# Letting the scan's tree stages in by VectorE's backlog, with ScalarE's bookings, two buffers, two loads and one product changed

## The chip, the cores and the metric

One core of a Trainium2 chip runs the kernel. The metric is the device time of one execution in microseconds; shorter is better. The engines are TensorE (PE, with PEld for its weight loads), VectorE (DVE), ScalarE (ACT), GpSimd (POOL) and the DMA queues, of which SyncE's (SP) carries nearly all loads.

## The reference

One encoder layer on 256 tokens with a model width of 2048, all in float32:

```python
h = rmsnorm(x, norm_mix_pre)
q_na, k_na, v_na, u_ssm, q_mem = split(h @ w_in)        # 1024, 1024, 1024, 512, 512 columns
y_na  = neighbourhood_attention(q_na, k_na, v_na, rpb)  # 8 heads x 128
y_ssm = s5_mixer(u_ssm, ...)                            # 32 groups x 64 complex states, forward and backward
y_mem = memory_cross_attention(q_mem, mem, mem_norm, w_mem_kv)   # 4 heads x 128, 256 memory tokens
y = concat(rmsnorm(y_na), rmsnorm(y_ssm), rmsnorm(y_mem))
x = x + rmsnorm(y @ w_out, norm_mix_post)
x = x + rmsnorm(square(relu(rmsnorm(x, norm_mlp_pre) @ w_ff1)) @ w_ff2, norm_mlp_post)   # hidden 8192
```

`s5_mixer` scans `h[t] = a * h[t-1] + b u[t]` over the tokens in both directions for each state, takes `Re(C h)` summed over the directions, adds `d * u`, and ends in a GELU and a gate `y * sigmoid(y @ w_glu + b_glu)` (the GLU).

## The kernel before

**The weight stream.** All weight matrices are cut into blocks of 128x128 and laid out in the order of use; eight blocks make a chunk (512 KB). For each chunk SyncE's queue loads `wraw`, ScalarE rounds it to the high part `wh` (`conv_high`), and VectorE subtracts to get the low part `wl` (`conv_low`). TensorE multiplies high by high, high by low and low by high. `take` (line 331) hands out blocks. At the start of a chunk it has the chunk two ahead converted (`AHEAD` = 2), and that in turn has a load issued; raw chunks have three buffers. Engines run their queues in order.

**The planner.** The kernel's Python code fixes the order of every queue while it writes the program. Side work (attention heads, the SSM, norms) is written as tasks, generators that issue a few instructions and then yield. `book` (line 109) keeps a clock for VectorE ("V"), GpSimd ("G"), ScalarE ("A") and TensorE ("E"), to which each instruction adds a booked cost (the `call` in `Engine`, line 128). `tick` (line 243), called at the start and in the middle of each chunk, goes through the tasks by priority and lets one step as long as it is due and each engine that it uses is booked less than `BACK` ns ahead of TensorE. `drain` forces a task to its end where its result is needed at once.

**The SSM** (lines 500 to 880). `lam_task` makes the discretised eigenvalues and their powers on VectorE and GpSimd. For each of four groups of channels `ut`, `b_task` runs `prep_b`, which makes powers of B (tile `W`, one buffer), transposes them (`wx`, `W1T`) and has `incr` multiply them with the inputs; the result for direction `d` is written to `XS`, and (`ut`, `d`) joins `xs_part`. `c_task` runs `prep_c`: it loads `Cw`, makes powers of C on VectorE and copies them to `CC` on ScalarE. `k0_task` then issues small matmuls on `CC`. `tree_task` runs `tree` twice, for groups 0 and 1 and for groups 2 and 3. A tree is the scan, in place in `XS`, in eleven stages of four VectorE instructions; the stages at level `l` touch columns that lie 2 to the power `l` + 1 apart, and their width falls from 32 columns to 1 and grows again. `ssm_task` issues the output matmuls and the GELU of each group (`ssm_out`) and then `yH` and `yL`, the GLU's input, which must be there after the first of four column groups of the output projection.

In the kernel before, the buffer with tag `ps` serves both `Cw` and the tree's temporary. `in_c` and `in_tree` keep `c_task` and `tree_task` from running together.

**The norm after the mix.** Near 440 us `r1`, the reciprocal root, is made (`rsqrt_pool`). `x1_part` adds the normed projection `acc1` to `x1` in column parts: on VectorE for the first 256 columns, and on ScalarE (product) and GpSimd (sum) for the others, the last quarter eight steps later. `gpost` holds the norm's weights, with which GpSimd multiplies `acc1`, quarter by quarter.

Of the kernel before, what the change touches and what calls it, by code (L numbers as in the profile page):

```python
# [41 lines left out]
SH_G = 500.0  # L42
BACK_V, BACK_G, BACK_A = 2600.0, 4000.0, 2200.0
WARM0, WARM1 = 7, 10
# [57 lines left out]
def hybrid_kernel(ctx: ExitStack, tc: tile.TileContext, A: dict, out: bass.AP, dbg=None):  # L102
# [16 lines left out]
    class Engine:  # L119
# [3 lines left out]
        def __getattr__(self, name):  # L123
# [3 lines left out]
            def call(o, *a, **kw):  # L127
# [11 lines left out]
                elif name == "tensor_reduce":  # L139
                    c = 80 + 1.04 * a[0].shape[1] * a[0].shape[2]  # L140
                elif e == "A":
                    c = 100 + 0.83 * n + (95 if any(isinstance(x, bass.AP) for x in kw.values()) else 0)
                elif e == "V":
                    c = (72 if n > 64 else 140) + n * {"tensor_copy": 0.52, "reciprocal": 8.0, "tensor_tensor_scan": 1.04,
                                   "tensor_scalar": 0.76, "memset": 0.3}.get(name, 1.04)
                else:
                    c = 155 + n * {"tensor_scalar": 0.9, "memset": 0.0, "tensor_copy": 1.6}.get(name, 2.1)
# [73 lines left out]
    tasks = []  # L221
    BACK = dict(V=BACK_V, G=BACK_G, A=BACK_A)

# [19 lines left out]
    def tick():  # L243
        for t in list(tasks):
            more = t[2] <= clk["E"]
            while more and all(clk[e] - clk["E"] < BACK[e] for e in t[3]):
                more = step(t)
# [444 lines left out]
    def incr(ut, d, wt):  # L692
# [8 lines left out]
        c0 = 8 * (ut % 2) + 4 * d  # L701
        o = XS[ut // 2][:, :, c0:c0 + 4, :]
        act(o[:, :, :, ::-1] if d else o, X)
        xs_part.add((ut, d))
# [7 lines left out]
    def prep_c(ut):  # L712
        cw = a2.tile([128, 4, 2, 8, 16], F32, name="Cw", tag="ps", bufs=1)
        nc.sync.dma_start(cw[:, 0], A["c"][:, ut])
# [37 lines left out]
    def tree(g):  # L752
# [3 lines left out]
        for up, l in [(1, l) for l in range(LEV)] + [(0, l) for l in range(LEV - 2, -1, -1)]:  # L756
# [3 lines left out]
            dst, src = X[:, :, :, d0::2 * h], X[:, :, :, d0 - h:NB - h:2 * h]  # L760
            t = a2.tile([128, 2, 16, NB // 2], F32, name="ps", tag="ps", bufs=1)[:, :, :, 0:n]
            tt(V, t, src[:, ::-1], pw[:, l, 0:2, cols][:, :, :, None].to_broadcast([128, 2, 16, n]), mult)
            tt(V, dst, dst, t, add)
# [55 lines left out]

    in_c, in_tree = [], []  # L820

    def b_task():
# [4 lines left out]
    def c_task():  # L827
        yield from until(lambda: lam_done)
        for ut in range(4):
            yield from until(lambda: not in_tree and (ut < 2 or ut - 2 in out_done))  # L830
            in_c.append(ut)
            yield from prep_c(ut)
            prepc.add(ut)
            in_c.clear()

    def tree_task():
        for g in range(2):
            yield from until(lambda: pw_done and not in_c and (2 * g + 1, 1) in xs_part and len(prepc) >= 2)
            in_tree.append(g)
            yield from tree(g)  # L840
            in_tree.clear()
            trees.add(g)
# [67 lines left out]
    for ut in range(2):  # L910
        load_b(ut)
    spawn(lam_task("V"), 2, "V")
    spawn(b_task(), 3, "VA")
    spawn(c_task(), 3, "VA")
    spawn(k0_task(), 3, "VA")
    spawn(tree_task(), 4, "V")
    st = spawn(ssm_task(), 5, "GA")
# [288 lines left out]
    rsqrt_pool(r1, v1)  # L1206
    for t in range(2):
        a = acc1[:, t, quarter(3)]
        tt(G, a, a, gpost[3], mult)
    B = ExitStack()  # L1210
# [4 lines left out]
    def x1_part(c):  # L1215

        for t in range(2):
            if c.stop <= 256:
                stt(x1[:, t, c], acc1[:, t, c], r1[:, t:t + 1], x1[:, t, c], mult, add)
            else:  # L1220
                act(acc1[:, t, c], acc1[:, t, c], AF.Copy, scale=r1[:, t:t + 1])
                tt(G, x1[:, t, c], x1[:, t, c], acc1[:, t, c], add)
# [270 lines left out]
```

## Time and profile before

| | |
|---|---|
| median of 3 runs | 1174.77 us (1172.07 to 1175.4) |
| the profiled execution | 1176.17 us, of which the span from first to last instruction is 1174.4 |
| TensorE busy | 1129.9 us, 96% of the span |
| VectorE busy | 718.5 us, 61% |
| ScalarE busy | 588.7 us, 50% |
| GpSimd busy | 97.7 us, 8% |
| mean granted TensorE clock | 0.987 of full speed |

The span falls into the first projection (to about 60 us), the memory keys and values (to about 114), the attention projections with the SSM beside them (to about 335), the output projection (to 440) and the MLP. A row of the timeline has the start, the duration, the engine, the instruction, what it writes and reads, and in brackets how long the engine sat idle before it and what ended that.

### The profile page before, as it was taken

What the parts mean: (1) busy time and instruction counts of PE and PEld (TensorE: products, weight loads), DVE (VectorE), ACT (ScalarE), POOL (GpSimd) and SP (SyncE); (2) the same over time, 40 slices, a digit from 0 to 9 for tenths busy, and PEclk for the clock granted to TensorE, in tenths of its full rate; (3) what the DMA queues carried; (4) which work ended last, traced back from release to release, by engine and by line L of the source; (5) the groups of instructions that cost most, each with busy time, mean ns of one, the idle gap of its engine ahead of it and who ended that gap; (6) DMA issues with size and microseconds to landing.
All of it is one profiled execution on the core that took longest, in us unless ns stands there. A gap on an engine that the chain in (4) does not pass through costs nothing.

```text
span 1174.4 us, 17404 instructions
## 1 busy us (share of the span) xinstructions
PE 1129.9 (96%) x6776; PEld 976.4 (83%) x6776; DVE 718.5 (61%) x1060; ACT 588.7 (50%) x908; POOL 97.7 (8%) x161
## 2 busy tenths in 40 slices
PE   8989896999989998999999999999999999999996
PEld 7978796989878887888888888888888888888885
DVE  6767498566966766676665444445666665445454
ACT  5677643566455546555455434343444544344342
POOL 1750000010000034000000000000000000011011
PEclk9999998999999999999999999999999999999998
DMA  8875353344444684666666666666666666666673
GB/s 285 303 218 171 109 162 104 100 131 138 154 127 142 187 280 145 182 190 188 195 187 189 186 191 184 191 185 192 189 190 194 186 192 184 193 193 197 189 210 127
DMA packets 62723, 213.05 MB, mean 181 GB/s; under 512 B 7216, under 2 KB 8752, under 8 KB 62640
## 3 DMA queue, kind: packets, MB, share of 16 engines
q1 hardware_dynamic: 62352, 211.84, 58.6%
q8 instruction: 53, 0.87, 0.3%
q14 instruction: 30, 0.25, 0.1%
q10 hardware_dynamic: 288, 0.09, 0.0%
HBM read 209.81 MB, written 2.10 MB: 180 GB/s over the span
## 4 chain that ended last, share of the span: by engine, by line
PE 72%; DVE 3%; issue 1%; ACT 1%; POOL 0%; DVEq 0%; ACTq 0%; POOLq 0%
PE acc L149 66%; PE big L149 5%; PE att L149 2%; DVE wl L149 1%; DVE ps L149 1%; DVE XS L149 1%; POOL x L149 0%; DVE facc L149 0%; ACT CC L149 0%; ACT wh L149 0%; DVE mn L149 0%; DVE rt L149 0%; DVE P L149 0%; DVE r L149 0%; ACT yH L149 0%
## 5 line engine op out<-in xcount | busy, mean ns | idle before, releaser
L149 DVE TENSOR_TENSOR wl<-wraw,wh 128x1024 fp32r<-128x1024 f32 (+1 forms) x372 | 454.2, 1225 | 389.2 <-ACT wh L149 389.0
L149 ACT ACTIVATE wh<-wraw 128x1024 fp32r<-128x1024 f32 (+1 forms) x372 | 391.2, 1054 | 419.4 <-PE acc L149 303.5
L149 PE MATMUL acc<-hs,wh 128*128 128x512 f32 (+1 forms) x996 | 346.4, 391 | 0.0
L149 PE MATMUL acc<-hs,wl 128*128 128x256 f32 x992 | 279.8, 283 | 0.0
L149 PEld LDWEIGHTS acc<-hs,wh 128*128 128x128 f32 x996 | 187.1, 188 | 38.6 <-ACT hs L149 0.2
L149 PEld LDWEIGHTS acc<-hs,wl 128*128 128x128 f32 x992 | 187.9, 190 | 0.0
L149 PE MATMUL acc<-wh,fH 128*128 128x512 f32 x448 | 178.8, 399 | 0.0
L149 PE MATMUL acc<-wh,fL 128*128 128x512 f32 x448 | 176.7, 394 | 0.0
L149 PE MATMUL acc<-wl,fH 128*128 128x512 f32 x448 | 175.7, 392 | 0.0
L149 PEld LDWEIGHTS acc<-wh,fL 128*128 128x128 f32 x448 | 84.1, 188 | 21.8
L149 PEld LDWEIGHTS acc<-wl,fH 128*128 128x128 f32 x448 | 84.1, 188 | 20.1
L149 PEld LDWEIGHTS acc<-wh,fH 128*128 128x128 f32 x448 | 84.1, 188 | 19.2
L149 PE MATMUL acc<-xH,wl 128*128 128x256 f32 x256 | 74.8, 292 | 9.3 <-DVE wl L149 9.2
L149 PE MATMUL acc<-xH,wh 128*128 128x256 f32 x256 | 77.2, 301 | 4.4 <-ACT wh L149 4.4
L149 PE MATMUL acc<-xL,wh 128*128 128x256 f32 x256 | 74.0, 289 | 0.0
L149 PEld LDWEIGHTS acc<-xH,wl 128*128 128x128 f32 x256 | 50.6, 198 | 10.6 <-DVE wl L149 10.6
L149 PEld LDWEIGHTS acc<-xH,wh 128*128 128x128 f32 x256 | 50.8, 199 | 5.2 <-ACT wh L149 4.6
L149 PEld LDWEIGHTS acc<-xL,wh 128*128 128x128 f32 x256 | 50.7, 198 | 0.4
L149 POOL TENSOR_TENSOR facc<-facc,g 128x512 f32<-128x512 f32 x6 | 10.1, 1710 | 475.5 <-DMA g<-in_g_dram 475.5
L149 PE MATMUL acc<-wh,mixn 128*128 128x512 f32 x128 | 40.8, 396 | 0.0
L149 ACT ACTIVATE P<-P,mn 128x256 f32<-128x256 f32 x24 | 12.0, 501 | 40.8 <-DVE mn L149 40.8
L149 DVE TENSOR_TENSOR XS<-XS,ps 128x32 f32<-128x32 f32 (+9 forms) x44 | 29.1, 661 | 1.5
(305 smaller groups left out, 1503.0 us busy)
## 6 DMA issues: line engine op xcount, KB each, us to landing
wraw<-in_w_dram SPq DMA_DIRECT2D x369, 512.0 KB, 4.3
tokst<-in_xt_dram SPq DMA_DIRECT2D x4, 512.0 KB, 7.9
mst<-in_memT_dram SPq DMA_DIRECT2D x4, 512.0 KB, 4.6
tokst<-in_mt_dram SPq DMA_DIRECT2D x4, 512.0 KB, 6.3
bias<-in_bias_dram SPq DMA_DIRECT2D x8, 256.0 KB, 4.0
x<-in_xt_dram SPq DMA_DIRECT2D x8, 256.0 KB, 5.9
out_dram<-facc SPq DMA_DIRECT2D x8, 256.0 KB, 2.4
xst<-in_xT_dram SPq DMA_DIRECT2D x7, 256.0 KB, 7.4
```

Source lines behind the costliest of these rows:

```text
L149: return f(o, *a, **kw)
```

## The change

- A tree stage may enter while VectorE is booked less than 1700 ns ahead (`BACK_TREE`, key `v`) instead of 2600, and stages above level 0 book `4 * 32 * n` ns more, `n` being their columns.
- ScalarE's booked costs go up: 205 ns instead of 100 per instruction, 80 for a scale from memory or a bias, 186 for an accumulator. Its limit `BACK_A` goes from 2200 to 3000.
- For groups 2 and 3 `Cw` lies in the buffer of `W`, `c_task` waits for (3,1) in `xs_part`, and the exclusion of `c_task` and `tree_task` is gone.
- The loads of B for groups 0 and 1 are issued ahead of the weights of chunks 5 and 6 instead of ahead of everything.
- The last quarter's product with `gpost[3]` moves from two GpSimd instructions into `x1_part`, where VectorE multiplies by `r1` and `gpost[3]` at once in place of ScalarE's product by `r1`.
- The output of `act` in `incr` is written in another form with the same meaning.

```diff
-BACK_V, BACK_G, BACK_A = 2600.0, 4000.0, 2200.0
+BACK_V, BACK_G, BACK_A, BACK_TREE = 2600.0, 4000.0, 3000.0, 1700.0
...
                 elif e == "A":
-                    c = 100 + 0.83 * n + (95 if any(isinstance(x, bass.AP) for x in kw.values()) else 0)
+                    c = (205 + 0.83 * n + (80 if isinstance(kw.get("scale"), bass.AP) or "bias" in kw else 0)
+                         + (186 if "accum_out" in kw else 0))
...
-    BACK = dict(V=BACK_V, G=BACK_G, A=BACK_A)
+    BACK = dict(V=BACK_V, G=BACK_G, A=BACK_A, v=BACK_TREE)
...
-            while more and all(clk[e] - clk["E"] < BACK[e] for e in t[3]):
+            while more and all(clk[e.upper()] - clk["E"] < BACK[e] for e in t[3]):
...
-        o = XS[ut // 2][:, :, c0:c0 + 4, :]
-        act(o[:, :, :, ::-1] if d else o, X)
+        act(XS[ut // 2][:, :, c0:c0 + 4, ::-1 if d else 1], X)
...
-        cw = a2.tile([128, 4, 2, 8, 16], F32, name="Cw", tag="ps", bufs=1)
+        cw = a2.tile([128, 4, 2, 8, 16], F32, name="Cw", tag="ps" if ut < 2 else "W", bufs=1)
...
             t = a2.tile([128, 2, 16, NB // 2], F32, name="ps", tag="ps", bufs=1)[:, :, :, 0:n]
+            if l:
+                book("V", 4 * 32 * n)
...
-            yield from until(lambda: not in_tree and (ut < 2 or ut - 2 in out_done))
-            in_c.append(ut)
+            yield from until(lambda: ut < 2 or ut - 2 in out_done and (3, 1) in xs_part)
...
-            yield from until(lambda: pw_done and not in_c and (2 * g + 1, 1) in xs_part and len(prepc) >= 2)
-            in_tree.append(g)
+            yield from until(lambda: pw_done and (2 * g + 1, 1) in xs_part and len(prepc) >= 2)
...
     for ut in range(2):
-        load_b(ut)
+        at(before_dma, 5 + ut, load_b, ut)
...
-    spawn(tree_task(), 4, "V")
+    spawn(tree_task(), 4, "v")
...
     rsqrt_pool(r1, v1)
-    for t in range(2):
-        a = acc1[:, t, quarter(3)]
-        tt(G, a, a, gpost[3], mult)
...
-                act(acc1[:, t, c], acc1[:, t, c], AF.Copy, scale=r1[:, t:t + 1])
+                if c.start >= 1536:
+                    stt(acc1[:, t, c], acc1[:, t, c], r1[:, t:t + 1], gpost[3], mult, mult)
+                else:
+                    act(acc1[:, t, c], acc1[:, t, c], AF.Copy, scale=r1[:, t:t + 1])
```

## Rows read from the trace of the kernel before

**Rows 1.** Waits of TensorE in the whole span: total, times, longest, in us.

```profile
PE acc L149 <- DVE wl L149: 12.7, 10, 3.6
```

**Rows 2.** Busy time by stage; columns PE, PEld, DVE, ACT, POOL, clock, DMA.

```profile
60.00:150.00 90.00, 82.57 (x538) 70.67 (x537) 58.93 (x124) 64.71 (x125) 15.64 (x48) 0.98 0.52 160
150.00:200.00 50.00, 39.59 (x300) 37.92 (x299) 48.33 (x73) 23.10 (x39) 0.73 (x1) 0.92 0.41 127
200.00:285.00 85.00, 82.65 (x825) 75.97 (x824) 46.78 (x95) 51.96 (x102) 6.59 (x9) 0.97 0.41 128
285.00:334.00 49.00, 43.54 (x319) 41.33 (x316) 47.10 (x68) 21.97 (x41) 0.74 (x1) 0.97 0.43 144
```

**Rows 3.** Timeline of TensorE: its longest waits between 60 and 440 us.

```profile
136.28 0.91 PE L149 MATMUL att<-CC,W 128*32 128x96 f32 x32 [2.53 <-issue]
...
193.84 0.58 PE L149 MATMUL acc<-xH,wh 128*128 128x256 f32 x1 [4.36 <-ACT wh L149]
...
198.27 0.58 PE L149 MATMUL acc<-xH,wl 128*128 128x256 f32 x1 [3.64 <-DVE wl L149]
...
265.59 0.91 PE L149 MATMUL att<-CC,W 128*32 128x96 f32 x32 [2.35 <-ACT CC L149]
...
325.15 0.54 PE L149 MATMUL acc<-xH,wl 128*128 128x256 f32 x1 [3.33 <-DVE wl L149]
```

**Rows 4.** Busy time and granted clock (third column from the end) behind two waits.

```profile
198.30:202.40 4.10, 4.10 (x19) 4.10 (x20) 2.33 (x4) 1.71 (x4) 0.00 (x0) 0.51 0.59 197
267.40:270.70 3.30, 3.30 (x15) 3.01 (x14) 0.00 (x0) 3.25 (x9) 0.00 (x0) 0.51 0.39 130
```

**Rows 5.** Timeline of ScalarE in the first tree.

```profile
191.74 0.51 ACT L149 ACTIVATE P<-P,mn 128x256 f32<-128x256 f32 x1 [9.99 <-DVE mn L149]
...
192.74 2.94 ACT L149 ACTIVATE wh<-wraw 128x1024 fp32r<-128x1024 f32 x3
```

**Rows 6.** Timeline of VectorE in the first tree.

```profile
191.62 1.18 DVE L149 TENSOR_TENSOR ps<-XS,pw 128x992 f32<-128x992 f32 x1
...
197.00 3.49 DVE L149 TENSOR_TENSOR wl<-wraw,wh 128x1024 fp32r<-128x1024 f32 x3
```

**Rows 7.** The page's costliest groups: busy us, mean ns; half of both trees.

```profile
L149 DVE TENSOR_TENSOR XS<-XS,ps 128x32 f32<-128x32 f32 (+9 forms) x44 | 29.1, 661 | 1.5
```

**Rows 8.** Groups of instructions by shape, VectorE, 60 to 380 us: a narrower stage.

```profile
L149 DVE TENSOR_TENSOR ps<-XS,pw 128x512 f32<-128x512 f32 x4 | 4.3, 1084 | 0.1
```

**Rows 9.** The chain that ended last: start, us, what.

```profile
272.78 11.45 PE acc L149 x96
```

**Rows 10.** Groups of instructions by shape, ScalarE, whole span.

```profile
L149 ACT ACTIVATE wh<-wraw 128x1024 fp32r<-128x1024 f32 x369 | 389.8, 1058 | 419.1 <-PE acc L149 303.5 <-issue 70.1 <-DMA wraw<-in_w_dram 33.7
```

**Rows 11.** Timeline of ScalarE: the last increment, (3,1), is written.

```profile
272.81 0.60 ACT L149 ACTIVATE XS<-att 128x512 f32<-128x512 f32 x1 [1.64 <-PE att L149]
```

**Rows 12.** Timeline of VectorE: the last instruction of the second tree.

```profile
331.13 1.19 DVE L149 TENSOR_TENSOR XS<-XS,ps 128x992 f32<-128x992 f32 x1
```

**Rows 13.** Timeline of TensorE: the GLU begins.

```profile
376.92 0.39 PE L149 MATMUL acc<-yH,wl 128*128 128x256 f32 x1 [0.39 <-DVE wl L149]
```

**Rows 14.** Timeline of SyncE's DMA queue: its first row.

```profile
0.72 0.86 SPq L648 DMA_DIRECT2D W<-in_b_dram  x2
```

**Rows 15.** The chain that ended last, from 446 us on.

```profile
446.49 1.43 POOL x L149 x2
```

**Rows 16.** Timeline of all engines ahead of the MLP.

```profile
441.24 0.16 DVE L149 TENSOR_TENSOR rt<-ry 128x2 f32<-128x2 f32 x1 [0.84 <-POOL ry L149]
441.31 2.48 POOL L149 TENSOR_TENSOR acc<-acc,gpost 128x512 f32<-128x512 f32 x2
441.44 1.15 DVE L149 SCALAR_TENSOR_TENSOR rt<-rt,v 128x2 f32<-128x2 f32 x1
442.62 1.19 DVE L149 SCALAR_TENSOR_TENSOR r<-rt,ry 128x2 f32<-128x2 f32 x1
...
444.25 1.26 PE L149 MATMUL att<-ident,x 128*128 128x128 f32 x4 [2.94 <-DVE x L149]
```

**Rows 17.** Timeline of GpSimd: the last quarter's sums.

```profile
465.54 2.54 POOL L149 TENSOR_TENSOR x<-x,acc 128x512 f32<-128x512 f32 x2 [6.72 <-ACT acc L149]
```

## What the change is expected to do

> **What bounds the kernel now.** I read first who TensorE waited for [rows 1], then its busy time by stage [rows 2], then the long waits one by one [rows 3], then the granted clock behind them [rows 4]. The reader should see that TensorE is the bound and that it waits mostly for `wl`, the low parts that VectorE makes. Its idle time by stage is 90.00 − 82.57 = 7.4 us in 60 to 150 us, 10.4 us in 150 to 200, 2.4 us in 200 to 285 and 5.5 us in 285 to 334 [rows 2]. The two stretches with the most idle time are those in which VectorE is full: 48.33 of 50 us and 47.10 of 49 us. Between them, from 200 to 285 us, VectorE is busy for only 46.78 of 85 us [rows 2]. VectorE's work is not too much; it lies badly.
>
> The two full stretches are the two runs of `tree`. The chain in the first is short to follow. A ScalarE softmax instruction waits 9.99 us for the minimum `mn`, which stands behind tree stages in VectorE's queue; the conversions `wh` of three chunks stand behind it on ScalarE and start only at 192.74 us [rows 5]. On VectorE a whole tree stage (four instructions from 191.62 us) comes next and the three `wl` start at 197.00 us [rows 6]. TensorE, two chunks on, waits 4.36 us and then 3.64 us; in the second tree 3.33 us [rows 3]. After these waits the granted clock is 0.51, the lower of the two levels (1.2 GHz), for 4.1 us with TensorE busy throughout; there are five such stretches, of 3.3 to 4.1 us, each behind a wait [rows 4].
>
> **Why the trees pile up.** The planner lets a tree stage in while VectorE's booked backlog is under 2600 ns. A stage is four instructions, booked at 72 + 1.04 n each (140 where n is at most 64). For n = 512 that is 604 ns, and the trace has 1084 [rows 8]. (This n counts elements; the code's own counts columns, 32 elements each.) Summing the eleven stages (n = 1024, 512, 256, 128, 64, 32, 32, 96, 224, 480, 992), the booking is 20.0 us a tree. The trace has 29.1 us for half of the instructions of both trees, the other half having the same shapes, so about 29 us a tree [rows 7]. Some 9 us a tree are on VectorE and in no booking.
>
> **Trees (line 762 and the gate).** The added booking is 128 ns per column for every level but 0; the columns of those stages sum to 57, so 7.3 us, and a tree is booked at 27.2 us: 2 us short instead of 9. A stage is now let in under 1700 ns. Bound for what stays: a chunk takes about 2.8 us of TensorE (24 matmuls; 96 of them took 11.45 us [rows 9]), and `wl` is wanted two chunks, 5.6 us, after it is queued. In the worst case a stage enters half a chunk (1.4 us) ahead of that: 1.7 + 4 × 1.23 − 1.4 + 1.23 = 6.5 us, so 0.7 us late allowing 0.2 us for the matmuls ahead of the first `wl`. The 512 and 480 stages come to about 0.2 us. Four of each kind give at most 3.6 us, at least nothing. What can go: 10.4 + 5.5 us of idle [rows 2], and of the lower clock about half of 4.1 us and half of an alike stretch of 3.3 us behind 325.15 us, 3.6 us; 19.5 us in all. I take 17.5, near the middle of 15.9 and 19.5.
>
> **ScalarE's bookings and BACK_A.** Two waits stand at `k0` (2.53 and 2.35 us [rows 3]): its matmuls are queued when the planner thinks the C powers are copied into `CC`, and ScalarE is later than booked. Booking 105 ns more for each plain instruction and 186 for an accumulator moves `k0` back by perhaps 1 us. With the clock behind them (half of 3.4 us and of 3.3 us) these waits cost 4.9 + 3.3 = 8.2 us. Between 0 and 8.2 I take 3.0: the planner also books these small matmuls too dear on TensorE, and that is not touched. BACK_A rises from 2200 to 3000, so with the new bookings steps come in about as often as before.
>
> **The C powers in the B buffer** (tag `W` for groups 2 and 3). `c_task` and `tree_task` no longer shut each other out, but `c_task` must now wait for the last increment, (3,1). Before, that increment was written at 272.81 us [rows 11], and the second tree, which needs it too, had to wait further for C. Cost: no instruction more or fewer. The load of `Cw` on SP's queue waits for the last reader of `W`, which (3,1) already implies; weights queued behind it have three raw buffers of lead. I book it at 0, covered by that lead; uncovered, it would be one `Cw` copy, about 2 us. The rewritten `act` of `XS` is the same instruction: 0.
>
> **The SSM loads moved.** The two loads of B hold SP's queue for 0.86 us ahead of the first x and weights [rows 14]; they return behind chunks 4 and 5, with data that `prep_b` uses only once the eigenvalues are made. Gain between 0 (the loads are paid again while the DMA queues are still busy) and 0.9 us; I take 0.3.
>
> **The last norm weights.** Two GpSimd products (2.48 us) start at 441.31 us. Beside them two VectorE instructions of 128x2 take 1.15 and 1.19 us, and they are the path to `x` and to TensorE's 2.94 us wait [rows 16]; one of the same size just before takes 0.16 us. Without the products they save 1.15 + 1.19 − 2 × 0.16 = 2.0 us. The lower clock behind the wait (3.3 us) is worth up to 1.6 us more, but GpSimd's sums for x follow [rows 15] and would bind part of it. I take 2.4, between 2.0 and 3.6. What is added: for the last quarter two VectorE instructions over 512 columns take the place of two ScalarE ones, near 465 us, where GpSimd then makes two sums in 2.54 us [rows 17]. The two chunks of lead hide this; uncovered it costs up to one such sum, 1.3 us.
> The Trainium skill, "SBUF — State Buffer", section "Who interferes with whom", says that a VectorE instruction with two SBUF inputs and a GpSimd one that reads SBUF exclude each other for a whole instruction. The trace agrees here: the two slow instructions end about where the two products end. By the same rule the change brings a new clash at 465 us, as its VectorE product has two SBUF inputs; by it one GpSimd sum, 1.3 us, would be added on that path, and if nothing hid it the gain would be 1.3 us less.
>
> **New waits.** Every step of the middle lands elsewhere. The row for what unplanned landings cost is the stage from 60 to 150 us: 7.4 us less the `k0` wait of 2.5, so 4.9 us. Between −2 and +4.9 us I take +3.5.
>
> **Sum.** 17.5 + 3.0 + 2.4 + 0.3 − 3.5 = 19.7 us. The profiled execution took 1176.2 us, its span 1174.4 and 1.8 around it, so 1156.5 by its scale. It stood 1.4 us above the median of the three runs, 1174.8; on that scale 1155.
>
> **Rivals.** *A, the waits move rather than go.* Stages still come whole, attention may enter ahead of them at 2600, and `k0` keeps its wait. Then 3.6 us of tree waits stay with one stretch of lower clock (1.7), the `k0` gain is 0 and new waits take 7: 14.2 + 2.4 − 7 = 9.6, about 1165. For it: attention's minima still queue behind tree stages. Against: the bookings come close to the traced durations.
>
> *B, the SSM chain comes late to the GLU; the slower side.* The second tree ended at 332.3 us [rows 12], and the GLU's first `wl` matmul started 44.6 us later with a wait of 0.39 us [rows 13]: the chain arrived just in time. With some 17 us of waits gone, TensorE reaches that place near 360 us, so a second tree that ends after 315 us makes it wait, one for one. To be slower than before it must end after about 335 us. A tree stage is now the last thing VectorE takes. Where no tree ran, other work took 55% of it [rows 2]; 45% left makes a 30 us tree last 67 us: 150 to 217, and if the second follows at once, 284 us. That needs (3,1) by 217 instead of 273 us. It is likely, since B's steps now go ahead of the trees and ScalarE's larger limit lets them in. If (3,1) stays near 256 us, the second tree ends near 323 and costs 8 us: 1163. If in addition the gate starves it by 20 us, 1183.
>
> *C, ScalarE is overbooked.* Three `wh` in a row took 2.94 us, 0.95 us from start to start [rows 5], though one is 1058 ns [rows 10]. The old booking, 950 ns, was the interval; the new one, 1055, is the duration. Where ScalarE is nearly full (64.71 of 90 us in 60 to 150 [rows 2]) 125 instructions at 0.1 us would hold the SSM's preparation back by up to 12 us. Nothing waits for that unless it reaches the GLU: from 284 to 296 us, still before 315. It would leave more C and B work beside the trees, about 5 us: 1160.
> The Trainium skill, "ScalarE: Activation LUTs", section "What ACT_TABLE_LOAD costs", gives the same overlap, some 93 ns for instructions back to back; by it the new bookings are too dear in a row, and the time would be C's.
>
> **How the numbers follow.** Forecast 0.60 (1147 to 1163), A 0.17, B 0.10 (slower in over half), C 0.08, and 0.05 that nearly all of the waits go (below 1147). The range 1147 to 1170 leaves out about 0.05 below and 0.12 above. Runs of this kernel can tell about 0.3% (3.5 us): faster 0.85, within it 0.06, slower 0.09.
>
> **What would show it.** Right: in the stretches of the trees TensorE idles under 5 us in sum and is never at 0.5 clock; VectorE is busy about alike from 150 to 290 us; the second tree starts before 240 us; `rt` and `r` take 0.16 us each and the wait for `x` falls to about 1 us. Wrong: tree stages back to back without a `wl` among them; a wait of several us for `yH` or `yL` ahead of the GLU; more or longer waits for `CC`, `wx` or `W1T`.

## The result: 12 us faster, most of it idle time ahead of the GLU

The changed kernel takes 1162.84 us (median; 1157.93 to 1164.31), the kernel before 1175.09 beside it: a ratio of 0.9893, 95% interval 0.9859 to 0.9928. The profiled execution took 1162.1 us, its span 1160.3; before it was 1176.2 and 1174.4. The helper line that stands for nearly every instruction is L149 before and L150 in the changed kernel.

Busy time by stage, as in [rows 2], and the whole way to the GLU's first matmul (columns PE, PEld, DVE, ACT, POOL, clock, DMA), changed kernel:

```profile
60.00:150.00 90.00, 86.96 (x585) 75.74 (x584) 58.60 (x117) 69.03 (x130) 15.28 (x43) 1.00 0.57 177
150.00:200.00 50.00, 48.30 (x383) 46.60 (x382) 43.09 (x71) 30.31 (x65) 1.09 (x1) 1.00 0.49 156
200.00:285.00 85.00, 81.09 (x773) 74.05 (x772) 70.62 (x125) 41.77 (x76) 7.18 (x9) 0.94 0.40 120
285.00:334.00 49.00, 45.76 (x277) 40.87 (x277) 37.32 (x52) 28.75 (x56) 2.51 (x3) 0.97 0.51 155
60.00:364.25 304.25, 289.29 (x2400) 259.62 (x2399) 224.24 (x397) 186.57 (x354) 29.07 (x61) 0.97 0.48 147
```

The same way in the kernel before, from 60 us to its GLU:

```profile
60.00:376.14 316.14, 290.49 (x2412) 261.30 (x2410) 224.26 (x401) 187.83 (x357) 29.02 (x66) 0.97 0.45 140
```

The GLU begins 11.9 us earlier, 364.25 instead of 376.14 (timeline of TensorE, before; [rows 13] is a little further on):

```profile
376.14 0.28 PE L149 MATMUL acc<-yH,wh 128*128 128x256 f32 x1
```

TensorE's idle time on the way fell from 25.65 to 14.96 us, that is by 10.7, and its busy time by 1.2. The 1.2 us are about what the start explains: in this pair of executions the changed kernel is 1.3 us ahead when it enters this way (its 361st weight matmul starts at 52.90 us, before at 54.18), and the trace has 12 matmuls fewer on it. From the GLU to the transposes of `x` another 2.0 us went (68.11 to 66.10), behind them 0.2: 14.1 us between the two profiled executions. From 150 to 200 us TensorE idles 1.70 us instead of 10.4, and VectorE is no longer full there: its busy share is 86% from 150 to 200, 83% from 200 to 285 and 76% from 285 to 334.

TensorE's waits, the first rows of the view that stands in [rows 1] (total, times, longest):

```profile
PE acc L150 <- DVE wl L150: 5.8, 6, 2.8
PE att L150 <- POOL sum_mo L150: 2.7, 1, 2.7
PE att L150 <- ACT CC L150: 2.5, 1, 2.5
```

The wait for `wl` fell from 12.7 to 5.8 us [rows 1]. All five long waits of [rows 3] are gone; three others stand in their place (timeline of TensorE):

```profile
239.84 1.02 PE L150 MATMUL att<-ones,sum_mo 128*128 128x1 f32 x4 [2.74 <-POOL sum_mo L150]
240.72 3.65 PE L150 MATMUL att<-U,W1T 128*128 128x64 f32 x16
...
297.13 0.58 PE L150 MATMUL acc<-xH,wl 128*128 128x256 f32 x1 [2.78 <-DVE wl L150]
...
347.69 0.35 PE L150 MATMUL att<-CC,W 128*32 128x96 f32 x5 [2.52 <-ACT CC L150]
```

Busy time and granted clock (third column from the end) behind the first two, as in [rows 4]:

```profile
239.90:249.90 10.00, 10.00 (x155) 9.88 (x158) 7.88 (x18) 2.15 (x4) 0.56 (x1) 0.53 0.40 134
297.20:300.60 3.40, 3.40 (x14) 3.19 (x15) 3.15 (x5) 0.00 (x0) 0.00 (x0) 0.52 0.66 173
```

So the lower clock did not go: over all microseconds between 60 us and the GLU, the time at 0.5 sums to 17.1 us, where it was 20.5. Of the 20.5 us TensorE was idle for 5.5, in its waits, and busy for 15.0; now it is busy for 16.1 of 17.1. What its matmuls pay for the lower clock has not fallen.

Where the wait at 239.84 us comes from is read backwards in the timeline of VectorE, ScalarE and GpSimd, changed kernel. `mixm` is the output of the memory attention, `sq` its square and `sum_mo` the sum of the squares, from which its norm is made:

```profile
235.78 1.19 DVE L150 TENSOR_TENSOR XS<-XS,ps 128x992 f32<-128x992 f32 x1
236.89 1.22 DVE L150 TENSOR_TENSOR wl<-wraw,wh 128x1024 fp32r<-128x1024 f32 x1
238.03 0.47 DVE L150 SCALAR_TENSOR_TENSOR mixm<-att,vecs,mixm 128x256 fp32r<-128x256 f32 x1
238.60 0.38 ACT L150 ACTIVATE sq<-att 128x256 f32<-128x256 f32 x1 [4.14 <-DVE mixm L150]
239.06 0.72 POOL L150 TENSOR_TENSOR sum_mo<-sum_mo,sq 128x256 f32<-128x256 f32 x1 [13.34 <-ACT sq L150]
```

`mixm` stands on VectorE behind a whole tree stage (232.09 to 236.97 us) and a `wl`. ScalarE waits 4.14 us for it with `sq`, GpSimd for `sq`, TensorE for GpSimd's sum. It is the pattern of the first tree before [rows 5, 6]: ScalarE waits in order for something that VectorE makes after a tree stage. The wait for `wl` at 297.13 us has it too (ScalarE, then VectorE, changed kernel):

```profile
291.75 0.51 ACT L150 ACTIVATE P<-P,mn 128x256 f32<-128x256 f32 x1 [3.71 <-DVE mn L150]
...
292.75 2.94 ACT L150 ACTIVATE wh<-wraw 128x1024 fp32r<-128x1024 f32 x3
...
294.92 1.03 DVE L150 TENSOR_TENSOR XS<-XS,ps 128x480 f32<-128x480 f32 x1
295.86 1.22 DVE L150 TENSOR_TENSOR wl<-wraw,wh 128x1024 fp32r<-128x1024 f32 x1
```

A softmax instruction waits 3.71 us for a minimum behind one stage, and three `wh` stand behind it. When the first of them is done, near 293.8 us (292.75 and about 1.06), VectorE is in the next stage (480 elements, from 291.63 us), so that `wl` starts some 2 us later still.

The last increment and the second tree come earlier than before, yet `yH` now comes later to the GLU than it did (timelines of ScalarE, VectorE, TensorE; compare [rows 11 to 13]; the last row is of the kernel before):

```profile
244.41 0.60 ACT L150 ACTIVATE XS<-att 128x512 f32<-128x512 f32 x1 [2.96 <-PE att L150]
...
313.36 1.19 DVE L150 TENSOR_TENSOR XS<-XS,ps 128x992 f32<-128x992 f32 x1
...
363.69 1.71 ACT L150 ACTIVATE yH<-uT,half 128x256 fp32r<-128x256 f32 x4 [1.33 <-DVE half L150]
...
364.25 0.39 PE L150 MATMUL acc<-yH,wh 128*128 128x256 f32 x1 [0.54 <-ACT yH L150]
...
372.94 1.71 ACT L149 ACTIVATE yH<-uT,half 128x256 fp32r<-128x256 f32 x4 [3.94 <-DVE half L149]
```

Before, `yH` was begun 3.2 us ahead of the GLU, 40.6 us behind the second tree; now it is begun 0.6 us ahead, 49.1 us behind the tree, and TensorE waits 0.54 us for it. The fourth C powers, copied at 281 us before, are copied only at 346.

The first tree now runs from 163 to 237 us and the second from 245 to 314.5; before they ran from 150 to 196 and from 285 to 332. The norm ahead of the MLP (compare [rows 16, 17]):

```profile
429.36 0.16 DVE L150 TENSOR_TENSOR rt<-ry 128x2 f32<-128x2 f32 x1 [0.84 <-POOL ry L150]
429.56 0.16 DVE L150 SCALAR_TENSOR_TENSOR rt<-rt,v 128x2 f32<-128x2 f32 x1
429.75 0.16 DVE L150 SCALAR_TENSOR_TENSOR r<-rt,ry 128x2 f32<-128x2 f32 x1
...
430.35 1.11 PE L150 MATMUL att<-ident,x 128*128 128x128 f32 x4 [0.92 <-DVE x L150]
...
437.77 0.30 PE L150 MATMUL att<-ident,x 128*128 128x128 f32 x1 [1.17 <-DVE hs L150]
...
452.79 3.98 POOL L150 TENSOR_TENSOR x<-x,acc 128x512 f32<-128x512 f32 x2 [7.99 <-DVE acc L150]
```

### The profile page after: what moved, and what is told of

It is laid out like the page before. It is cut to its first block, busy times and chain, and to the rows that moved or that the text cites. A ratio compares the mean times of both kernels' runs of the same rounds, so it can differ in the third digit from the quotient of the medians.

```text
span 1160.3 us, 17398 instructions
## 1 busy us (share of the span) xinstructions
PE 1128.0 (97%) x6776; PEld 974.4 (84%) x6776; DVE 719.6 (62%) x1062; ACT 587.0 (51%) x906; POOL 96.8 (8%) x159
## 4 chain that ended last, share of the span: by engine, by line
PE 80%; DVE 7%; ACT 4%; DMA 3%; POOL 3%; issue 3%; SPq 0%; DVEq 0%; ACTq 0%; POOLq 0%
PE acc L150 70%; PE big L150 5%; PE att L150 5%; DVE wl L150 3%; DMA wraw<-in_w_dram 3%; ACT wh L150 2%; DVE ps L150 1%; DVE XS L150 1%; ACT P L150 1%; POOL u L150 1%; DMA gpost<-in_post_dram 0%; POOL x L150 0%; POOL cs L150 0%; DVE mn L150 0%; DVE P L150 0%
## 5 line engine op out<-in xcount | busy, mean ns | idle before, releaser
L150 DVE TENSOR_TENSOR wl<-wraw,wh 128x1024 fp32r<-128x1024 f32 (+1 forms) x372 | 455.5, 1226 | 378.4 <-ACT wh L150 378.1
L150 ACT ACTIVATE wh<-wraw 128x1024 fp32r<-128x1024 f32 (+1 forms) x372 | 391.3, 1053 | 421.5 <-PE acc L150 291.0
L150 PE MATMUL acc<-hs,wh 128*128 128x512 f32 (+1 forms) x996 | 346.0, 391 | 0.0
L150 PE MATMUL acc<-hs,wl 128*128 128x256 f32 x992 | 279.3, 282 | 0.0
L150 PEld LDWEIGHTS acc<-hs,wh 128*128 128x128 f32 x996 | 186.6, 188 | 38.9 <-ACT hs L150 0.2
L150 PEld LDWEIGHTS acc<-hs,wl 128*128 128x128 f32 x992 | 187.3, 189 | 0.0
L150 PE MATMUL acc<-wh,fH 128*128 128x512 f32 x448 | 178.7, 399 | 0.0
L150 PE MATMUL acc<-wh,fL 128*128 128x512 f32 x448 | 176.5, 394 | 0.0
L150 PE MATMUL acc<-wl,fH 128*128 128x512 f32 x448 | 175.7, 392 | 0.0
L150 PEld LDWEIGHTS acc<-wh,fL 128*128 128x128 f32 x448 | 84.1, 188 | 22.0
L150 PEld LDWEIGHTS acc<-wl,fH 128*128 128x128 f32 x448 | 84.1, 188 | 19.9
L150 PEld LDWEIGHTS acc<-wh,fH 128*128 128x128 f32 x448 | 84.1, 188 | 19.3
L150 PE MATMUL acc<-xH,wl 128*128 128x256 f32 x256 | 72.7, 284 | 3.5 <-DVE wl L150 3.5
L150 PE MATMUL acc<-xH,wh 128*128 128x256 f32 x256 | 74.8, 292 | 0.0
L150 PE MATMUL acc<-xL,wh 128*128 128x256 f32 x256 | 72.2, 282 | 0.0
L150 PEld LDWEIGHTS acc<-xH,wl 128*128 128x128 f32 x256 | 48.8, 190 | 3.9 <-DVE wl L150 3.9
L150 PEld LDWEIGHTS acc<-xH,wh 128*128 128x128 f32 x256 | 48.8, 190 | 0.6
L150 PEld LDWEIGHTS acc<-xL,wh 128*128 128x128 f32 x256 | 48.8, 190 | 0.3
L150 POOL TENSOR_TENSOR facc<-facc,g 128x512 f32<-128x512 f32 x6 | 9.1, 1536 | 476.8 <-DMA g<-in_g_dram 476.8
L150 PE MATMUL acc<-wh,mixn 128*128 128x512 f32 x128 | 42.5, 408 | 0.0
L150 DVE TENSOR_TENSOR XS<-XS,ps 128x32 f32<-128x32 f32 (+9 forms) x44 | 30.2, 687 | 1.5
L150 PEld LDWEIGHTS acc<-wh,mixn 128*128 128x128 f32 x128 | 24.7, 193 | 6.2 <-issue 0.3
```

What stands on the lines that cost most here:

```text
L150: return f(o, *a, **kw)
```

## The experiments

Each run has its own runs of the kernel before beside it; the ratio is to those. The last two columns are of its profiled execution: TensorE's idle time from 60 us to the GLU's first matmul (length of the stretch less busy time), and the time at the lower clock in it (each microsecond counted by its granted clock). "Undone" means the changed kernel with that part as before; "alone" means the kernel before with that part; "limit" is `BACK_A` and "costs" are ScalarE's booked costs. The changed kernel itself has four runs and an interval of 0.7%, so differences to it of less than some 4 us are open.

| kernel | us | ratio, 95% interval | GLU begins | idle | lower clock |
|---|---|---|---|---|---|
| before | 1175.09 | 1 | 376.1 | 25.7 | 20.5 |
| changed | 1162.84 | 0.9893 (0.9859 to 0.9928) | 364.3 | 15.0 | 17.1 |
| trees alone | 1174.63 | 0.9996 (0.9985 to 1.0007) | 375.3 | 21.9 | 23.9 |
| norm weights alone | 1172.36 | 0.9977 (0.9966 to 0.9988) | 374.5 | 24.5 | 23.9 |
| ScalarE's part undone | 1173.11 | 0.9988 (0.9978 to 0.9998) | 376.1 | 23.0 | 23.9 |
| C part undone | 1168.11 | 0.9944 (0.9923 to 0.9964) | 369.5 | 21.4 | 18.2 |
| limit undone | 1197.33 | 1.0201 (1.0184 to 1.0218) | 395.1 | 45.6 | 42.6 |
| costs undone | 1161.49 | 0.9898 (0.9882 to 0.9914) | 363.1 | 14.6 | 13.6 |
| tree part undone | 1176.46 | 1.0023 (1.0013 to 1.0034) | 375.5 | 25.2 | 18.2 |
| memory norm late | 1158.54 | 0.9876 (0.9858 to 0.9894) | 360.8 | 14.0 | 10.2 |
| limit alone | 1181.94 | 1.0070 (1.0050 to 1.0090) | 381.4 | 25.4 | 30.7 |
| trees and limit | 1173.78 | 0.9998 (0.9984 to 1.0011) | 374.1 | 20.8 | 20.5 |
| limit 3800, old costs | 1170.53 | 0.9976 (0.9963 to 0.9989) | 372.5 | 19.8 | 23.8 |
| half stages | 1159.41 | 0.9876 (0.9860 to 0.9893) | 361.2 | 13.6 | 3.4 |

The theory at the start was the prediction's: the tree part carries nearly everything. The rivals: the parts carry it together, or another part does. In the edits, `...` stands for lines left out.

**Trees alone.** The kernel before with the gate and the added booking, nothing else:

```diff
-BACK_V, BACK_G, BACK_A = 2600.0, 4000.0, 2200.0
+BACK_V, BACK_G, BACK_A, BACK_TREE = 2600.0, 4000.0, 2200.0, 1700.0
...
-            while more and all(clk[e] - clk["E"] < BACK[e] for e in t[3]):
+            while more and all(clk[e.upper()] - clk["E"] < BACK[e] for e in t[3]):
...
+            if l:
+                book("V", 4 * 32 * n)
...
-    spawn(tree_task(), 4, "V")
+    spawn(tree_task(), 4, "v")
```

> The kernel before with the tree part alone: stages let in under 1700 ns, levels above 0 booked 128 ns per column dearer. Theory (VectorE's bookings carry the change): most of the gain of the middle, 7 to 12 us under the kernel before, so 1163 to 1168 us; no wait of TensorE over 3 us in the stretches of the trees. Rival (the C powers' own buffer, with tree and C no longer shut out from each other, carries it): under 3 us, 1172 us or more.

No gain: 1174.63 against 1174.87 of the kernel before. The waits moved. The first tree stretched to 160 to 225 us, but the second still began at 289 and ended at 357, and TensorE now waited for `W1T`, the transposed powers of B, with 6.8 us of lower clock behind it (timeline of TensorE, trees alone):

```profile
204.07 0.66 PE L149 MATMUL att<-U,W1T 128*128 128x64 f32 x4 [3.53 <-ACT W1T L149]
```

**Norm weights alone**, the kernel before with that part:

```diff
-    for t in range(2):
-        a = acc1[:, t, quarter(3)]
-        tt(G, a, a, gpost[3], mult)
...
-                act(acc1[:, t, c], acc1[:, t, c], AF.Copy, scale=r1[:, t:t + 1])
+                if c.start >= 1536:
+                    stt(acc1[:, t, c], acc1[:, t, c], r1[:, t:t + 1], gpost[3], mult, mult)
+                else:
+                    act(acc1[:, t, c], acc1[:, t, c], AF.Copy, scale=r1[:, t:t + 1])
```

> The kernel before with the last quarter's norm weights on VectorE alone. Theory: the two slow VectorE instructions ahead of x fall from 1.15 and 1.19 us to about 0.16 us each, TensorE's wait for x falls from 2.94 to about 0.95 us, and the time by 1.8 to 2.6 us (1172.5 to 1173.3). Rival (two SBUF inputs clash with GpSimd's sums at the last quarter): the gain is given back there, under 1 us in all.

1172.36 against 1174.87: 2.5 us, as the theory had it. `rt` and `r` take 0.16 us each, the wait for `x` is 0.93 us, and no lower clock stands behind it.

**ScalarE's part undone**: the changed kernel with the old costs and BACK_A 2200.

```diff
-BACK_V, BACK_G, BACK_A, BACK_TREE = 2600.0, 4000.0, 3000.0, 1700.0
+BACK_V, BACK_G, BACK_A, BACK_TREE = 2600.0, 4000.0, 2200.0, 1700.0
...
-                    c = (205 + 0.83 * n + (80 if isinstance(kw.get("scale"), bass.AP) or "bias" in kw else 0)
-                         + (186 if "accum_out" in kw else 0))
+                    c = 100 + 0.83 * n + (95 if any(isinstance(x, bass.AP) for x in kw.values()) else 0)
```

> The changed kernel with ScalarE's bookings and its limit of 2200 ns as before. Theory (VectorE's bookings carry the change, ScalarE's only shift positions): within 4 us of the changed kernel's 1163, either way. Rival C of the prediction (the new bookings are too dear in a row): 3 us or more faster, 1160 or less. Rival (they remove the waits for copies into CC): 4 to 8 us slower, 1167 to 1171, with a wait of about 2.5 us for CC near 136 us again.

1173.11: 10 us above the changed kernel, outside all three answers. With the trees alone giving nothing and this, the first theory fell: a part that was to be worth 3.0 us decides over 10. The increments are late ((2,0) in `XS` at 208 us instead of 176, (3,1) at 271 instead of 244), and the waits are those of the trees alone: 3.54 us for `W1T` at 203.91 us, and at 135.39 us the 2.53 us ahead of `k0`, the sign of the last answer.

**C part undone**: `Cw` in `ps` and the exclusion as before.

```diff
-        cw = a2.tile([128, 4, 2, 8, 16], F32, name="Cw", tag="ps" if ut < 2 else "W", bufs=1)
+        cw = a2.tile([128, 4, 2, 8, 16], F32, name="Cw", tag="ps", bufs=1)
...
-            yield from until(lambda: ut < 2 or ut - 2 in out_done and (3, 1) in xs_part)
+            yield from until(lambda: not in_tree and (ut < 2 or ut - 2 in out_done))
+            in_c.append(ut)
...
-            yield from until(lambda: pw_done and (2 * g + 1, 1) in xs_part and len(prepc) >= 2)
+            yield from until(lambda: pw_done and not in_c and (2 * g + 1, 1) in xs_part and len(prepc) >= 2)
```

> The changed kernel with Cw in the tree's buffer for all groups and with tree and C shut out from each other, as before. Theory: 0 to 4 us slower than the changed kernel (1163 to 1167), as the trees' bookings stay. Rival (this part carries the change): 6 us or more slower, 1169 or more. Second rival (waiting for the last increment makes the C powers of the last group late, which is what stands ahead of the GLU in the changed kernel): 1 to 4 us faster.

1168.11, between the first two answers: the part, booked at nothing, is worth 5.3 us by the medians, though the two intervals just touch (0.9923 and 0.9928). The second tree starts at 246 us, about as in the changed kernel (245), but now the C powers must wait until it ends at 298, and they are the last thing ahead of the GLU (timeline of TensorE, C part undone):

```profile
355.36 1.53 PE L150 MATMUL att<-CC,W 128*32 128x96 f32 x32 [3.31 <-ACT CC L150]
359.31 3.25 PE L150 MATMUL att<-uT,BD 128*128 128x192 f32 x12 [2.42 <-ACT BD L150]
369.47 0.58 PE L150 MATMUL acc<-yH,wh 128*128 128x256 f32 x1 [3.88 <-ACT yH L150]
```

**Limit undone**: only BACK_A back to 2200, the new costs stay.

```diff
-BACK_V, BACK_G, BACK_A, BACK_TREE = 2600.0, 4000.0, 3000.0, 1700.0
+BACK_V, BACK_G, BACK_A, BACK_TREE = 2600.0, 4000.0, 2200.0, 1700.0
```

> The changed kernel with ScalarE's limit alone set back (BACK_A 2200 instead of 3000); its new bookings stay. With both set back the time was 1173.1 us, 10 us above the changed kernel's 1162.8. Theory 1 (the limit carries the gain: with it, B's steps enter ahead of the first tree): 1171 to 1174 us, the group (2,0) is written to XS after 200 us and TensorE again waits 2 to 3.5 us for wl and W1T. Theory 2 (the bookings carry it, as they bring ScalarE's clock to its traced durations): 1162 to 1165, (2,0) near 176 us as in the changed kernel. If both are needed, 1167 to 1172, with one of the two waits back.

1197.33, far outside what either theory expected: 34.5 us slower than the changed kernel. Dearer bookings under an unchanged limit leave the tasks of B too few steps. The last increment is at 318.69 us (ScalarE), the second tree ends at 368.6 us (VectorE), and TensorE stands still for it and for what follows (TensorE); rows of the timeline, limit undone:

```profile
318.69 0.60 ACT L150 ACTIVATE XS<-att 128x512 f32<-128x512 f32 x1 [0.38 <-PE att L150]
...
367.40 1.19 DVE L150 TENSOR_TENSOR XS<-XS,ps 128x992 f32<-128x992 f32 x1
...
368.65 3.60 PE L150 MATMUL att<-XS,CC 128*32 128x63 f32 x128 [16.59 <-DVE XS L150]
381.56 1.53 PE L150 MATMUL att<-CC,W 128*32 128x96 f32 x32 [9.31 <-ACT CC L150]
```

**Costs undone**: only the old costs, the limit stays at 3000.

```diff
-                    c = (205 + 0.83 * n + (80 if isinstance(kw.get("scale"), bass.AP) or "bias" in kw else 0)
-                         + (186 if "accum_out" in kw else 0))
+                    c = 100 + 0.83 * n + (95 if any(isinstance(x, bass.AP) for x in kw.values()) else 0)
```

> The changed kernel with ScalarE's booked costs alone set back (100 + 0.83 n); the limit stays at 3000. Theory 1 (the limit carries the gain): 1162 to 1166 us, second tree starting before 255 us. Theory 2 (the bookings carry it): 1171 to 1174, with waits for W1T or CC of 2 to 3.5 us, because matmuls are queued before ScalarE has written what they read.

1161.49, not to be told from the changed kernel (0.9898 and 0.9893), so the first theory. Waits for `W1T` did come, as the second had it (2.85 us at 121.83 and 3.01 at 195.74), but others went. What ScalarE's part gives is its limit; the bookings at traced durations give nothing, and without the limit they cost 24 us more than the old ones (1197.3 against 1173.1).

**Tree part undone**: gate and added booking back, all else changed.

```diff
-            if l:
-                book("V", 4 * 32 * n)
...
-    spawn(tree_task(), 4, "v")
+    spawn(tree_task(), 4, "V")
```

> The changed kernel with the tree part set back: a stage may enter below 2600 ns again and books nothing extra. The prediction gave this part 17.5 us; the run with the tree part alone gained 0.2 us. If the part works only together with the others, this comes to 1170 to 1176 us, with waits of 3 to 4 us for wl behind tree stages, as in the kernel before. If the gain came from the other parts, 1161 to 1166, and the trees last under 50 us each.

1176.46, the first answer: among the other parts the tree part is worth 13.6 us, alone 0.2. The trees take 52 and 69 us, the second from 278 to 346, a wait behind a tree stage is back, and TensorE waits for the SSM chain ahead of the GLU (timeline of TensorE, tree part undone):

```profile
207.40 0.80 PE L150 MATMUL acc<-wl,xH 128*128 128x512 f32 x1 [2.68 <-DVE wl L150]
...
341.16 3.25 PE L150 MATMUL att<-uT,BD 128*128 128x192 f32 x12 [2.95 <-ACT BD L150]
```

**Memory norm late**: the norm of the memory attention's output let in 4 us later.

```diff
+        yield from after(4000.0)
         st_rx["mo"], _ = yield from rms([sums["mo"]], 1.0 / 512, "mo", bcast=False)
```

> The changed kernel with the norm of the memory attention's output let in 4 us of TensorE's time later, so that its matmul with the ones is queued later behind GpSimd's sum. In the changed kernel that matmul waits 2.74 us at 239.84 us and TensorE then runs at the lower clock for 10 us. If that wait is simply too early an issue: it falls below 1 us, the stretch of lower clock goes, and the time is 3 to 8 us less, 1155 to 1160. If the chain behind it (VectorE's mixm, ScalarE's square, GpSimd's sum) is late however late it is queued: the wait stays at 2 to 3 us and the time stays at 1162 to 1165.

Neither answer as put. The wait for `sum_mo` went, and a wait of 3.00 us for `W1T` took its place at once, with 6.8 us of lower clock: `W1T` stands on ScalarE behind the same `sq`, which waits for `mixm` behind the same tree stage (timeline of ScalarE and TensorE, memory norm late):

```profile
239.12 0.38 ACT L150 ACTIVATE sq<-att 128x256 f32<-128x256 f32 x1 [4.17 <-DVE mixm L150]
...
239.93 1.11 ACT L150 ACTIVATE W1T<-att 128x512 f32<-128x512 f32 x2
...
240.60 0.69 PE L150 MATMUL att<-U,W1T 128*128 128x64 f32 x2 [3.00 <-ACT W1T L150]
```

So the late chain, not the early issue, makes that wait. A wait of 2.74 us for `wl`, at 314.87 us, stays as well. In the order that followed, the fourth C powers are copied at 300 us instead of 346, and the 2.52 us wait at 347.69 is gone. The time, 1158.54 us, isn't settled against the changed kernel's: the intervals of the ratios overlap.

**Limit alone**: the kernel before with one number changed.

```diff
-BACK_V, BACK_G, BACK_A = 2600.0, 4000.0, 2200.0
+BACK_V, BACK_G, BACK_A = 2600.0, 4000.0, 3000.0
```

> The kernel before with one number changed: ScalarE's limit BACK_A 3000 instead of 2200; its booked costs and all else as before. Theory (limit and tree gate give their gain only together: the limit lets B's steps in early, the gate keeps the tree's stages from delaying wl): the limit alone gives little, 1171 to 1177 us; the steps of B come earlier than before ((2,0) in XS before 220 us, (3,1) before 260), but TensorE still waits 3 to 4 us for wl behind tree stages. Rival (the limit alone carries the gain, the trees have no part): 1162 to 1167.

1181.94, 8.3 us slower than the kernel before beside it (1173.66) and slower than either answer. B's steps do come early, the last increment at 242 us. But they bring ScalarE's work into the stretch in which whole tree stages enter at 2600 (timeline of ScalarE and TensorE, limit alone):

```profile
183.78 0.51 ACT L149 ACTIVATE P<-P,mn 128x256 f32<-128x256 f32 x1 [6.70 <-DVE mn L149]
...
184.78 1.06 ACT L149 ACTIVATE W1T<-att 128x512 f32<-128x512 f32 x2
...
185.40 0.90 PE L149 MATMUL att<-U,W1T 128*128 128x64 f32 x3 [5.79 <-ACT W1T L149]
```

The softmax waits 6.70 us for a minimum behind a tree stage, and `W1T`, a step of B let in early, waits with it.

**Trees and limit**: the kernel before with both.

```diff
-BACK_V, BACK_G, BACK_A = 2600.0, 4000.0, 2200.0
+BACK_V, BACK_G, BACK_A, BACK_TREE = 2600.0, 4000.0, 3000.0, 1700.0
...
+            if l:
+                book("V", 4 * 32 * n)
...
-    spawn(tree_task(), 4, "V")
+    spawn(tree_task(), 4, "v")
```

> The kernel before with the tree part (gate at 1700, added booking) and BACK_A 3000, and nothing else; ScalarE's costs, the C buffer, the SSM loads and the norm weights as before. The tree part alone came to 1174.6. Theory (the two work together): 1164 to 1168 us, that is the changed kernel without its C part (5.3 us by the run with C undone) and without the norm weights (2.5) and with nothing from ScalarE's costs. If the C part is needed as well for any gain: 1170 to 1175, with C's powers late and a wait of 2 to 4 us for CC or yH ahead of the GLU.

1173.78: the second answer. The trees are done by 282 us, earlier than in the changed kernel, but C is shut out meanwhile and copied only at 312 and 347 us, and `BD`, made from it, is late (timeline of TensorE, trees and limit):

```profile
322.15 1.03 PE L149 MATMUL att<-uT,BD 128*128 128x192 f32 x5 [2.12 <-ACT BD L149]
```

Set side by side, with the old costs and without the norm weights (their 2.5 us added where a run has them):

| parts | us | from |
|---|---|---|
| none | 1174.8 | before |
| trees | 1174.6 | trees alone |
| limit | 1181.9 | limit alone |
| trees and limit | 1173.8 | trees and limit |
| trees and C | 1175.6 | ScalarE's part undone, plus 2.5 |
| limit and C | 1179.0 | tree part undone, plus 2.5; with the new costs |
| all three | 1164.0 | costs undone, plus 2.5 |

Of these only all three together gain; the C part alone was not run.

**Limit 3800**, old costs, the rest as changed.

```diff
-BACK_V, BACK_G, BACK_A, BACK_TREE = 2600.0, 4000.0, 3000.0, 1700.0
+BACK_V, BACK_G, BACK_A, BACK_TREE = 2600.0, 4000.0, 3800.0, 1700.0
```

> The changed kernel with ScalarE's booked costs as before and its limit raised further, 3800 instead of 3000. At 2200 the time was 1173.1 us, at 3000 it was 1161.5. Theory (what the limit gives is B's early start, and at 3000 the second tree already ends 75 us ahead of the GLU): nothing more to gain, 1159 to 1166; W1T and wx waits may grow, as ScalarE's queue is longer. Rival (the gain goes on with the limit): 1152 to 1158.

1170.53, worse than both answers. The second tree is done at 304 us, so B's early start is there; the loss is again `W1T` behind ScalarE's wait for `mixm` and for a minimum: 3.30 us at 169.96 and 2.97 at 200.51, with about 7 us of lower clock behind each.

**Half stages**: the changed kernel, a tree stage let in by halves.

```diff
             if l:
-                book("V", 4 * 32 * n)
+                book("V", 2 * 32 * n)
             tt(V, t, src[:, ::-1], pw[:, l, 0:2, cols][:, :, :, None].to_broadcast([128, 2, 16, n]), mult)
             tt(V, dst, dst, t, add)
+            yield True
+            if l:
+                book("V", 2 * 32 * n)
             tt(V, t, src, pw[:, l, 2, cols][:, None, :, None].to_broadcast([128, 2, 16, n]), mult)
```

> The changed kernel with each tree stage let in by halves: two of its four instructions, then the gate (1700 ns) is asked again, and each half books its own share of the addition. In the changed kernel whole stages of up to 4.9 us still stand ahead of wl and mixm: TensorE waits 2.74 us at 239.84 (mixm, through ScalarE's square and GpSimd's sum) and 2.78 us at 297.13 (wl), with 10 and 3.4 us of the lower clock behind them. Theory (the whole stage is the cause): both waits fall below 1 us, the trees last longer but the second ends before 335 us, and the time is 1153 to 1159. Rival (any new order brings other waits of the same size, as in the runs with the limit at 3800 and with the memory norm late): the two waits go but others of 2 to 3 us come, at W1T, CC or wl; 1159 to 1170.

1159.41, at the border of the two ranges, and the second tree ends at 342 us, later than the theory had it; the waits decide for the theory. In the timeline of VectorE `mixm` now stands between the halves of a stage:

```profile
233.56 1.06 DVE L150 TENSOR_TENSOR XS<-XS,ps 128x480 f32<-128x480 f32 x1
234.51 0.49 DVE L150 SCALAR_TENSOR_TENSOR mixm<-att,vecs,mixm 128x256 fp32r<-128x256 f32 x1
234.90 1.06 DVE L150 TENSOR_TENSOR ps<-XS,pw 128x480 f32<-128x480 f32 x1
```

No wait for `wl` is longer than 0.8 us, the wait for `sum_mo` is 0.68, and the clock on the way to the GLU is 0.99 (waits of TensorE; busy time and clock, half stages):

```profile
PE acc L150 <- DVE wl L150: 6.0, 9, 0.8
...
60.00:361.18 301.18, 287.54 (x2414) 255.26 (x2412) 225.91 (x400) 185.40 (x355) 32.67 (x70) 0.99 0.48 149
```

No wait of 2 us or more is left between 60 us and the GLU, and a single stretch of 3.4 us at the lower clock. It beats the kernel before by 1.2%. Against the changed kernel the medians differ by 3.4 us and the profiled spans by 2.9 (1160.3 and 1157.4), but the intervals overlap (0.9860 to 0.9893, 0.9859 to 0.9928): that it beats both is likely and not settled.

## Why the prediction was right, and where its steps were not

The time lies within the range, 7.8 us above the forecast of 1155 and nearer to the numbers of rivals C (1160) and A (1165). The direction and the reason in outline held: TensorE's waits behind the tree stages were the cost, VectorE's work was evened out, and the waits went. The sum was 5.6 us too high (19.7 against 14.1 between the two profiled executions), and two of its terms, the trees' taken alone and ScalarE's, are wrong by more than that. That it came so near is in part luck: the trees' 17.5 us need the limit and the C part, which stand in the sum with 3.0 and 0, and the new waits were booked too small.

- **Trees, 17.5 us: not a term of its own.** Alone the part gives 0.2 us, among the others 13.6. The step that failed is the bound for what stays: 0.7 us at `wl` for a full stage, 0.2 for one of 512 or 480 elements, 3.6 in all. It counted one stage ahead of `wl` alone. The trace shows 5.5 us: 2.78 at one `wl`, behind a stage of 480, and 2.74 through `mixm`, ScalarE and GpSimd: where a stage delays something that ScalarE waits for in order, everything behind it on ScalarE is late too. The prediction describes this chain in the kernel before and leaves it out of its bound. In the half stages both waits went and no other of 2 us came, as this account has it; that run's time is not settled against the changed kernel's.
- **The lower clock, 3.6 us of that term.** None of it came: TensorE's busy time at the lower clock was 15.0 us and is 16.1, because one new wait brought 10 us of it.
- **ScalarE, 3.0 us.** Both waits at `k0` did go. It did not take the dearer bookings: with the costs undone no wait at `k0` is longer than 0.65 us. And a third, of 2.52 us at 347.69 us, came for the late C powers. The sentence that with the higher limit steps come in about as often as before is wrong: the limit carries the part, and B's last increment came 28.4 us earlier (272.81 to 244.41). The bookings give nothing that the runs can tell at a limit of 3000, and cost 24 us at 2200.
- **C in the B buffer, 0 us.** Measured 5.3, with intervals that touch, through the exclusion, whose end was named in that step and not priced: with the trees early and long, C would have been last.
- **SSM loads, 0.3 us.** The runs can't tell. The 361st weight matmul starts at 52.97 us in the mean of nine profiles with the loads moved (51.97 to 54.66) and at 53.63 in five without (52.42 to 54.33).
- **Last norm weights, 2.4 us: right**, 2.5 measured. The lower clock's 1.6 us did not come on top: from the transposes of `x` to the next wait for `hs` it takes 7.5 us before (444.25 to 451.79) and 7.4 after. The matmuls in it are done sooner (TensorE is busy for 6.2 us instead of 7.3), but the wait for `hs` grew from 0.26 to 1.17 us: the time to the next `hs` did not shrink with them. The two sums of the last quarter took 3.98 us instead of 2.54 [rows 17], behind 7.99 us of idle time, and TensorE did not wait there. The first took 1.75 us, beside the second of VectorE's new products; the other came to stand beside a `wl` (454.14 to 455.61 us), which is no part of the change. By the Trainium skill, "SBUF — State Buffer", section "Who interferes with whom", a VectorE instruction with two SBUF inputs contends with a GpSimd instruction that reads SBUF. The trace agrees, with 1.44 us more beside two such instructions, but only a part of it is the clash which the prediction priced at 1.3 us.
- **New waits, 3.5 us.** Too small. The three new waits are 8.0 us, with the lower clock behind each, outside the range of −2 to +4.9; two of them are the trees' of the first point, the third is the 2.52 us at `k0`. The row it was sized by, the stage from 60 to 150 us, holds no tree.
- **Rivals.** A named what happened to the trees: minima and products behind whole stages. B had the geometry: it put the point from which the second tree costs at 315 us and the GLU near 360; the tree ended at 314.5, between its two cases (284 and 323), and the GLU began at 364.25. Its reading that the chain arrived just in time before is not in its row: the 0.39 us of [rows 13] are a wait for `wl`, and `yH` was begun 3.2 us ahead. The run with the limit undone is B in full, 2% slower. C's harm is real under the old limit (24 us, that run); at 3000 the old costs give the same time (1161.49 and 1162.84 us), so the change doesn't pay C's 5 us. The Trainium skill, "ScalarE: Activation LUTs", section "What ACT_TABLE_LOAD costs", says that instructions back to back overlap. The trace agrees, three `wh` in a row again take 2.94 us, but the time did not become C's by it.
- **What would show it.** `rt`, `r` and the wait for `x` came as said, VectorE was evened out, but the second tree began at 245 us, not before 240. Under 5 us of idle time in the trees' stretches was missed: 163.1 to 237.0 and 245.0 to 314.5 us hold 2.9 and 2.8 us, and the 2.74 us behind the first tree's last stage fall just between the two. The clock did fall to 0.5 in the second.

## What to carry to other kernels

Price a wait at the end of the whole in-order chain: what stands behind the delayed instruction on each further engine, not only the operand that was late before. Where a planner lets work in by several limits, their parts don't add: undo each from the whole and do each alone before giving any of them a number, and when a booked cost is raised, ask what its limit then admits. Cutting the unit that is let in took away the waits here which a tighter gate only moved.

## What the runs showed that was not expected

The stretch at the lower clock behind a wait isn't of one length. Counted as in the table it is 3.4 us behind the `wl` wait at 297.13 us, 6.8 behind the wait for `W1T` with trees alone, and 10.2 behind the 2.74 us wait for `sum_mo`, though TensorE is then busy for 10.00 of 10.00 us. What TensorE runs next doesn't settle it. In the two longer ones the SSM's narrow matmuls (16 of 64 columns) come first, but with C undone the same wait of 2.74 us, with the same matmuls behind it, has 6.8 us, and with the costs undone the 16 narrow matmuls behind a wait of 3.01 us for `W1T` have 3.4. What sets the length isn't shown.

In the half stages TensorE's busy time at the lower clock is 3.4 us instead of the changed kernel's 16.1, and yet its busy time to the GLU is only 1.8 us less. Part of that is the start: the half stages are 1.8 us behind (361st weight matmul at 54.66 instead of 52.90 us) and their trace has 14 matmuls more on the way. The rest isn't shown.
